# Score and mask matmuls of a recurrence over 128 rows instead of 64 and 40

## The chip, the core and the metric

The kernel runs on one core of a Trainium2 chip. The metric is the device time of one execution in microseconds (us). TensorE (PE in the profile) does the matmuls, VectorE (DVE), ScalarE (ACT) and GpSimd (POOL) the rest; SyncE (SP) issues most DMAs. A matmul has a stationary operand, which a weight load (PEld) puts into the array, and a moving one, whose columns stream past it; it contracts over the rows (partitions) that both operands occupy, 128 at most.

## The reference, cut to what matters

Two transformer blocks follow each other (512 tokens, width 1024, float32). The change lies in the first mixer of the first block, a gated recurrence (mLSTM) with 8 heads, query and key width 64, value width 128:

```python
def mlstm_chunkwise(q, k, v, i_pre, f_pre):
    logf = jax.nn.log_sigmoid(gate(f_pre))
    ig = gate(i_pre)
    b = jnp.cumsum(logf, axis=-1)
    ...
    D = jnp.where(causal, b[..., :, None] - b[..., None, :] + ig[..., None, :], -jnp.inf)
    m_t = jnp.maximum(b_inter, jnp.max(D, axis=-1))
    P = jnp.exp(D - m_t[..., None]) * jnp.einsum('bhctk,bhcsk->bhcts', q, k)
    ...
    h = num / jnp.maximum(jnp.abs(den), jnp.exp(-m_t))[..., None]
```

Queries and keys are projections of the input that go through a causal convolution of four taps and a SiLU. A second mixer (stick-breaking attention), the output projection and an MLP end the first block; a sparse attention is the second.

## The kernel before, in words

The kernel treats the recurrence as one masked attention over all 512 tokens, without chunks. A head's scores, transposed (key s in the rows, query t in the columns), come in four key blocks `sb` of 128 rows and 512, 384, 256 and 128 columns. Float32 accuracy is had by splitting an operand into a rounded part and a rest. `qs` holds in 64 of its rows the head's rounded queries and in the other 64 the rests (L513, L514); `kh` holds the rounded keys twice (L515, L516); `kl` the rests of the keys, in 64 rows only (L517). A score block is two matmuls into one bank of PSUM: `kh` with `qs` over 128 rows (L529), then `kl` with the rounded queries over 64 rows (L530). The mask factor `E` is an exponential (L524) of a running maximum that is first spread over all partitions: a matmul over 40 rows (L519) of `mst`, whose rows 0 to 7 and 32 to 39 hold the maximum of the eight heads, rounded and rest, with a column of the selector `s8` repeated 128 times.

DVE multiplies scores and mask (L531, recorded at its helper's line L298); then follow 10 matmuls with the values per head (L544), DVE's copy of their sum (L546, in the trace "spare"), the norm (squares on ACT L549, a power on POOL and a product on DVE, both recorded at L301 as "mnr", a scaling on ACT L560) and a transposition (L484).

The loop runs over four pairs `j` of heads, `e` = 0 and 1 in each. A pair's projections (L341 to L343, 24 matmuls each for q and for k) stand on PE among the previous pair's scores, and during the last pairs those of the next mixer (L374 to L376). Each engine has its own queue and works it in order; Tile's scheduler set those orders when the kernel was built. Three steps bind them: the score blocks alternate between two banks (`sc2`), so a pair's third block waits for DVE's product on the first; a value sum takes the one bank `av`, so the next waits for the copy L546; the scores of a pair wait for ACT's copies of the keys (L515, L516), which stand behind convolution and SiLU. Weights come by DMA on SP's queue three tiles ahead.

`qs`, `kh`, `kl` of e = 0 are three tiles of the pool `pm`; those of e = 1 are slices of a tile `AT`, taken anew in each pair. The stores of the bias tables (L735, L736), of which the change's name speaks, stand on GpSimd's queue in this kernel already.

Of the kernel before, what the change touches and what calls it, by code (L numbers as in the profile page):

```python
# [8 lines left out]
F32 = mybir.dt.float32  # L9
F32R = mybir.dt.float32r  # L10
AF = mybir.ActivationFunctionType
OP = mybir.AluOpType
# [3 lines left out]
T = 512  # L16
# [237 lines left out]
def tile_blocks(ctx, tc, x, xt, wts, prm, cst, table, post_g, w2k, w2v, out):  # L254
    nc = tc.nc
    v, s, g, pe, sy = nc.vector, nc.scalar, nc.gpsimd, nc.tensor, nc.sync
# [17 lines left out]
    ident = glob.tile([128, 128], F32, name="ident")  # L274
# [10 lines left out]
    def col(base, k, rows=128):  # L285
        return pr[0:rows, base + k:base + k + 1]
# [10 lines left out]
    def stt(out_, a, sc, b, op0, op1):  # L297
        v.scalar_tensor_tensor(out_, a, sc, b, op0, op1)  # L298

    def tt(out_, a, b, op=OP.mult, eng=None):  # L300
        (eng or v).tensor_tensor(out_, a, b, op)  # L301
# [26 lines left out]
    def act_tiles(kt):  # L328
        h = glob.tile([128, T], F32R, name=f"ah{kt}", tag="ah", bufs=8)
        l = glob.tile([128, T], F32R, name=f"al{kt}", tag="al", bufs=8)  # L330
        return h, l
# [65 lines left out]
    def first_mixer():  # L397
        with tc.tile_pool(name="pa", bufs=1) as pa:
            pj, sc, mx, tp, av = ring(0, 1, 2, 3), ring(4), ring(5), ring(6), ring(7)
            acts = []  # L400
            for kt in range(KT):
                xk = pa.tile([128, T], F32, name="xk", tag="w2", bufs=2)
                sy.dma_start(xk, xt[128 * kt:128 * kt + 128, :])
                h, l = act_tiles(kt)
# [14 lines left out]
            with tc.tile_pool(name="pm", bufs=1) as pm:  # L419
# [6 lines left out]
                def values(h0, n, w):  # L426
                    def evac(tb, ps):
                        s.activation(VA[:, tb, h0:h0 + n, 0:128],
                                     ps[:, 0:128 * n].rearrange("p (a b) -> p a b", a=n), AF.Identity,
                                     scale=rs[:, tb:tb + 1])  # L430
                        if w > 128 * n:
                            s.activation(gt[:, tb, :].rearrange("p (a b) -> p a b", b=8)[:, 0:5:4, :],
                                         ps[:, 128 * n:128 * n + 16].rearrange("p (a b) -> p a b", a=2),
                                         AF.Identity, scale=rs[:, tb:tb + 1])
                    emit(gen_n(pj, acts, evac, w=w))
# [20 lines left out]
                um = pa.tile([40, T], F32, name="um", tag="ke", bufs=2)  # L456
# [2 lines left out]
                M = pa.tile([8, T], F32, name="M", tag="w2b", bufs=2)  # L459
                v.tensor_tensor_scan(M, um[0:8, :], um[0:8, :], 0.0, OP.max, OP.bypass)  # L460
                stt(um[32:40, :], F, -1.0, M, OP.mult, OP.subtract)
                mst = pa.tile([40, T], F32R, name="mst", tag="be", bufs=2)
                v.tensor_copy(mst, um)
                v.tensor_copy(mst[0:8, :], M)
                tt(mst[32:40, :], M, mst[0:8, :].bitcast(F32), OP.subtract)
                s8 = pa.tile([40, 8], F32R, name="s8")
                tt(s8, ident[0:40, 0:8], ident[0:40, 32:40], OP.add)
                values(6, 2, 256)
                pst = sc()
                for tb in range(4):  # L470
# [10 lines left out]
                def flip_head(h, num):  # L481
                    pst = tp()
                    for tb in range(4):
                        pe.transpose(pst[:, 128 * tb:128 * tb + 128], num[:, tb, 0:128], ident)  # L484
                    s.activation(ha[:, h, :], pst, AF.Identity, scale=col(P_GML, h))

                for j in range(4):
                    qk = []
                    for i in range(2):
                        ps = proj_t(pj3, acts)  # L490
                        xp = pm.tile([128, T + 4], F32, name="xp", tag="xp", bufs=2)
                        v.memset(xp[:, 0:3], 0.0)
                        tt(xp[:, 3:T + 3], ps, R)
                        y = pm.tile([128, T], F32, name="y", tag="cv", bufs=2)
                        cb = P_CONV + 4 * (4 * i + j)
                        s.activation(y, xp[:, 0:T], AF.Identity, scale=pr[:, cb:cb + 1])
                        for t in range(1, 4):
                            stt(y, xp[:, t:t + T], pr[:, cb + t:cb + t + 1], y, OP.mult, OP.add)
                        th = xp[:, 0:T]
                        s.activation(th, y, AF.Tanh, scale=0.5)  # L500
                        stt(y, th, 1.0, y, OP.add, OP.mult)
                        qk.append(y)
                    q_, k_ = qk
                    for e in range(2):
                        h = 2 * j + e
                        rows = slice(64 * e, 64 * e + 64)
                        other = slice(64 - 64 * e, 128 - 64 * e)
                        if e == 0:
                            qs, kh, kl = (pm.tile([128, T], F32R, name="st", tag=f"st{i}", bufs=1) for i in range(3))
                        else:  # L510
                            st = pa.tile([128, 4, T], F32R, name="AT", tag="AT", bufs=1)
                            qs, kh, kl = (st[:, i, :] for i in range(3))
                        s.copy(qs[rows, :], q_[rows, :])  # L513
                        tt(qs[other, :], q_[rows, :], qs[rows, :].bitcast(F32), OP.subtract)  # L514
                        s.copy(kh[rows, :], k_[rows, :])  # L515
                        s.copy(kh[other, :], k_[rows, :])  # L516
                        tt(kl[rows, :], k_[rows, :], kh[rows, :].bitcast(F32), OP.subtract)  # L517
                        mb = mx()
                        pe.matmul(mb, s8[:, h:h + 1].to_broadcast([40, 128]), mst, start=True, stop=True)  # L519
                        PT = []  # L520
                        for sb in range(4):
                            n = T - 128 * sb
                            E = pm.tile([128, n], F32, name="E", tag=f"E{sb}", bufs=2)
                            s.activation(E, mb[:, 128 * sb:T], AF.Exp, scale=-1.0, bias=un[:, sb, h:h + 1])  # L524
                            g.affine_select(E[:, 0:128], E[:, 0:128], pattern=[[1, 128]], compare_op=OP.is_ge,
                                            fill=0.0, base=0, channel_multiplier=-1)
                            S = sc2()
                            ks = slice(128 * sb, 128 * sb + 128)
                            pe.matmul(S[:, 0:n], kh[:, ks], qs[:, 128 * sb:T], start=True, stop=False)  # L529
                            last = pe.matmul(S[:, 0:n], kl[rows, ks], qs[rows, 128 * sb:T], start=False, stop=True)  # L530
                            stt(E, S[:, 0:n], 0.125 / 4, E, OP.mult, OP.mult)  # L531
                            PT.append(E)
                        if len(late) > LATE:
                            with tc.issue_after(last.ins):
                                flip_head(*late.pop(0))
                        num = spare[:, 516 * (h % NUMS):516 * (h % NUMS) + 516].rearrange("p (a b) -> p a b", a=4)
                        sq = small([128, 4], "sq")
                        for half in range(2):
                            o = av()
                            o2 = o[:, 0:258].rearrange("p (a b) -> p a b", a=2)  # L540
                            for i in range(2):
                                tb = 2 * half + i
                                for sb in range(tb + 1):
                                    pe.matmul(o2[:, i, :], PT[sb][:, 128 * (tb - sb):128 * (tb - sb) + 128],  # L544
                                              VA[:, sb, h, 0:129], start=(sb == 0), stop=(sb == tb))
                            v.tensor_copy(num[:, 2 * half:2 * half + 2, :], o2)  # L546
                        jk = glob.tile([128, 128], F32, name="jk", tag="dg", bufs=2)
                        for tb in range(4):
                            s.activation(jk, num[:, tb, 0:128], AF.Square, accum_out=sq[:, tb:tb + 1])  # L549
                        den = small([128, 4], "den")  # L550
                        stt(den, num[:, :, 128], -1.0, num[:, :, 128], OP.mult, OP.max)
                        tt(den, den, enm[:, :, h], OP.max)
                        v.reciprocal(den, den)
                        r2 = small([128, 4], "r2")
                        tt(r2, den, den)
                        tt(r2, r2, sq)
                        f = rsqrt_mean(r2, 128, "mn", 4)
                        tt(f, f, den)
                        for tb in range(4):
                            s.activation(num[:, tb, 0:128], num[:, tb, 0:128], AF.Identity, scale=f[:, tb:tb + 1])  # L560
                        late.append((h, num))
# [843 lines left out]
```

## Time and profile before

| what | value |
|---|---|
| time, median of 3 runs | 1387.51 us (1386.82 to 1389.72) |
| profiled execution, its own time | 1387.11 us |
| its span | 1385.2 us (mean granted clock 0.994) |
| PE busy | 1331.9 us, 96% |
| DVE busy | 809.2 us, 58% |
| ACT busy | 650.8 us, 47% |
| stretch of the recurrence's heads | 66.91 to 158 us |

The profile is of one execution; times in it are microseconds from the span's start. A matmul's end is modelled, and successive matmuls overlap in the records, so that pace is read from the differences of their starts.

### The profile page before, as it was taken

The numbers are of one execution on the slowest core, as the hardware profiler recorded it, in microseconds if no ns is written. First come the engines' busy times: TensorE is split into PE (matmuls) and PEld (weight loads), VectorE is DVE, ScalarE is ACT, GpSimd is POOL, SyncE is SP. The second block draws the span as 40 slices with busy tenths as digits, with TensorE's granted clock in tenths as the row PEclk, the third lists the DMA queues.
The fourth block names the chain that finished last, engine by engine and source line by source line (L and its number), as shares of the span: only waits on it lengthen the run. The fifth ranks groups of instructions, "written<-read, shape, count | busy, mean of one in ns | idle before, by whom it ended". The sixth has DMA issues, their size and how long they took to land.

```text
span 1385.2 us, 17815 instructions
## 1 busy us (share of the span) xinstructions
PE 1331.9 (96%) x6622; PEld 1087.3 (78%) x6622; DVE 809.2 (58%) x1596; ACT 650.8 (47%) x1273; POOL 264.5 (19%) x235
## 2 busy tenths in 40 slices
PE   9999999999999999999999999899788999999898
PEld 7977787868686888888888888788677878777776
DVE  4678535556667535342233323545988998988823
ACT  6577634443434326351135512344546656665522
POOL 0022101010101000000000000144536342323352
PEclk9999999999999999999999999999999999999999
DMA  7411221213121424762332234323223122121132
GB/s 236 135 43 49 61 92 61 91 47 97 56 91 48 149 78 132 117 187 91 97 100 92 96 100 124 111 61 121 84 63 111 50 61 68 48 70 47 52 122 76
DMA packets 40695, 125.31 MB, mean 90 GB/s; under 512 B 4528, under 2 KB 9184, under 8 KB 40352
## 3 DMA queue, kind: packets, MB, share of 16 engines
q1 hardware_dynamic: 39696, 119.98, 27.3%
q0 software_dynamic: 912, 4.19, 2.3%
q8 instruction: 52, 0.85, 0.3%
q14 instruction: 35, 0.29, 0.1%
HBM read 115.77 MB, written 8.39 MB: 90 GB/s over the span
## 4 chain that ended last, share of the span: by engine, by line
PE 60%; issue 15%; DVE 15%; ACT 5%; POOL 3%; DMA 1%; SPq 0%; POOLq 0%; DVEq 0%; ACTq 0%
PE b L375 9%; PE b L374 9%; PE b L376 9%; PE b L341 8%; PE b L342 8%; PE b L343 8%; DVE P L295 3%; DVE b L1173 2%; DVE ptall L301 2%; ACT wh L172 1%; PE b L824 1%; ACT P L1177 1%; PE b L1208 1%; PE b L544 1%; PE b L1192 1%
## 5 line engine op out<-in xcount | busy, mean ns | idle before, releaser
L172 ACT CAST wh<-wr 128x1024 fp32r<-128x1024 f32 (+3 forms) x204 | 207.9, 1020 | 399.0 <-PE b L376 223.4
L174 DVE TENSOR_TENSOR wl<-wr,wh 128x1024 fp32r<-128x1024 f32 (+2 forms) x142 | 169.5, 1195 | 296.8 <-ACT wh L172 296.4
L341 PE MATMUL b<-ah,wh 128*128 128x512 f32 x808 | 329.4, 408 | 0.4 <-DVE q L298 0.3
L343 PE MATMUL b<-ah,wl 128*128 128x512 f32 x808 | 317.5, 393 | 0.0
L342 PE MATMUL b<-al,wh 128*128 128x512 f32 x808 | 317.2, 393 | 0.0
L343 PEld LDWEIGHTS b<-ah,wl 128*128 128x128 f32 x808 | 152.2, 188 | 33.5 <-issue 0.8
L341 PEld LDWEIGHTS b<-ah,wh 128*128 128x128 f32 x808 | 152.5, 189 | 27.8 <-issue 1.0
L174 POOL TENSOR_TENSOR wl<-wr,wh 128x1024 fp32r<-128x1024 f32 (+1 forms) x62 | 143.6, 2320 | 157.7 <-ACT wh L172 148.0
L342 PEld LDWEIGHTS b<-al,wh 128*128 128x128 f32 x808 | 152.8, 189 | 24.1 <-issue 0.5
L374 PE MATMUL b<-wh,ah 128*128 128x512 f32 (+3 forms) x352 | 125.8, 359 | 1.4 <-ACT ah L308 0.9
L376 PE MATMUL b<-wh,al 128*128 128x512 f32 (+3 forms) x352 | 125.5, 357 | 0.1
L375 PE MATMUL b<-wl,ah 128*128 128x512 f32 (+3 forms) x352 | 125.3, 356 | 0.1
L1177 ACT ACTIVATE P<-b,nm 128x128 f32<-128x128 f32 (+3 forms) x128 | 67.5, 528 | 105.2 <-DVE nm L1173 102.8
L375 PE MATMUL b<-wl,hh 128*128 128x512 f32 x256 | 102.1, 399 | 0.0
L374 PE MATMUL b<-wh,hh 128*128 128x512 f32 x256 | 100.9, 394 | 0.0
L376 PE MATMUL b<-wh,hl 128*128 128x512 f32 x256 | 100.4, 392 | 0.0
L295 DVE TENSOR_SCALAR P<-P,rd,gn 128x128 f32<-128x128 f32 (+3 forms) x128 | 93.7, 732 | 2.4
L374 PEld LDWEIGHTS b<-wh,ah 128*128 128x128 f32 x352 | 66.2, 188 | 9.9 <-ACT ah L308 1.3
L376 PEld LDWEIGHTS b<-wh,al 128*128 128x128 f32 x352 | 66.4, 189 | 8.8 <-DVE al L298 0.5
L375 PEld LDWEIGHTS b<-wl,ah 128*128 128x128 f32 x352 | 66.4, 189 | 8.4 <-DVE wl L174 0.5
L1192 PE MATMUL b<-ident,P 128*128 128x128 f32 x320 | 56.7, 275 | 12.7 <-DVE ptall L301 10.4
L301 POOL TENSOR_TENSOR rsr<-rsm,mhalf 128x2 f32<-128x2 f32 (+1 forms) x3 | 2.4, 806 | 334.6 <-DVE rsm L295 334.6
(288 smaller groups left out, 2214.1 us busy)
## 6 DMA issues: line engine op xcount, KB each, us to landing
wr<-in_wts_dram SPq DMA_DIRECT2D x188, 512.0 KB, 3.6
bt_d<-tr POOLq DMA_DIRECT2D x4, 768.0 KB, 21.9
wr<-in_wts_dram SPq DMA_DIRECT2D x8, 280.0 KB, 2.6
xk<-in_xt_dram SPq DMA_DIRECT2D x8, 256.0 KB, 4.1
xn<-in_x_dram SPq DMA_DIRECT2D x4, 512.0 KB, 5.6
xbig<-in_x_dram SPq DMA_DIRECT2D x1, 2048.0 KB, 9.6
x_d<-xbig SPq DMA_DIRECT2D x8, 256.0 KB, 3.0
bt<-bt_d SPq DMA_DIRECT2D x8, 256.0 KB, 2.8
```

Source lines behind the costliest of these rows:

```text
L172: nc.scalar.copy(hi, raw)
L174: eng.tensor_tensor(lo, raw, hi.bitcast(F32), OP.subtract)
L295: (eng or v).tensor_scalar(out_, in_, s1, s2, op0, op1)
L301: (eng or v).tensor_tensor(out_, a, b, op)
L341: pe.matmul(o, a, ah, start=(kt == 0), stop=False)
L342: pe.matmul(o, a, al, start=False, stop=False)
L343: pe.matmul(o, b, ah, start=False, stop=(kt == KT - 1))
L374: pe.matmul(o, ah[:, tsl], a, start=(kk == 0 and k == 0), stop=False)
L375: pe.matmul(o, ah[:, tsl], b, start=False, stop=False)
L376: W.last = pe.matmul(o, al[:, tsl], a, start=False, stop=end)
L1177: latest[0] = s.activation(P[:, 0:n], S[:, 0:n], AF.Exp, bias=nm, scale=-1.0, accum_out=rd)
L1192: pe.transpose(pst[:, 128 * sb:128 * sb + 128], P[:, 128 * sb:128 * sb + 128], ident)
```

## The change

`mst` and `s8` become tiles of 128 rows; `mst` is set to zero once, rows 0 to 39 are then written as before, and the mask matmul contracts over all 128. `kl` becomes for each `e` one tile that lives through the whole loop: its 64 unused rows are set to zero once ahead of the loop, and the second score matmul takes all 128 rows of `kl` and `qs`. The tile `AT` is therefore taken once, ahead of the loop. Bias stores are where they were.

```diff
-                mst = pa.tile([40, T], F32R, name="mst", tag="be", bufs=2)
-                v.tensor_copy(mst, um)
+                mst = pa.tile([128, T], F32R, name="mst", tag="be", bufs=2)
+                v.memset(mst.bitcast(F32), 0.0)
+                v.tensor_copy(mst[0:40, :], um)
...
-                s8 = pa.tile([40, 8], F32R, name="s8")
-                tt(s8, ident[0:40, 0:8], ident[0:40, 32:40], OP.add)
+                s8 = pa.tile([128, 8], F32R, name="s8")
+                tt(s8, ident[:, 0:8], ident[:, 32:40], OP.add)
...
+                st = pa.tile([128, 4, T], F32R, name="AT", tag="AT", bufs=1)
+                kz = [pm.tile([128, T], F32R, name="kz"), st[:, 2, :]]
+                for e in range(2):
+                    v.memset(kz[e][64 - 64 * e:128 - 64 * e, :].bitcast(F32), 0.0)
...
-                            qs, kh, kl = (pm.tile([128, T], F32R, name="st", tag=f"st{i}", bufs=1) for i in range(3))
+                            qs, kh = (pm.tile([128, T], F32R, name="st", tag=f"st{i}", bufs=1) for i in range(2))
...
-                            st = pa.tile([128, 4, T], F32R, name="AT", tag="AT", bufs=1)
-                            qs, kh, kl = (st[:, i, :] for i in range(3))
+                            qs, kh = (st[:, i, :] for i in range(2))
+                        kl = kz[e]
...
-                        pe.matmul(mb, s8[:, h:h + 1].to_broadcast([40, 128]), mst, start=True, stop=True)
+                        pe.matmul(mb, s8[:, h:h + 1].to_broadcast([128, 128]), mst, start=True, stop=True)
...
-                            last = pe.matmul(S[:, 0:n], kl[rows, ks], qs[rows, 128 * sb:T], start=False, stop=True)
+                            last = pe.matmul(S[:, 0:n], kl[:, ks], qs[:, 128 * sb:T], start=False, stop=True)
```

PE's order of before, in the scores of head 0 (b_730 and b_737 are the score banks, b_896 the bank of a projection):

```order
389 L529 MATMUL b_730<-st 128x256
390 L530 MATMUL b_730<-st 128x256
391 L544 MATMUL b_742<-VA,E 128x129 x2
392 L529 MATMUL b_737<-st 128x128
393 L530 MATMUL b_737<-st 128x128
```

And the same place after the change, where a line's number is higher by six:

```order
389 L535 MATMUL b_734<-st 128x256
390 L536 MATMUL b_734<-st,kz 128x256
391 L550 MATMUL b_746<-VA,E 128x129 x2
392 L535 MATMUL b_741<-st 128x128
393 L536 MATMUL b_741<-st,kz 128x128
```

Nothing moves there: apart from the numbers of buffers and lines, PE's queue is the same from end to end, and so are those of ACT, POOL and SP. Only DVE's queue has new rows, at its start (al_94 is the rest of the first input tile):

```order
5 L457 MEMSET um 40x512
6 L463 MEMSET mst 128x512
7 L491 MEMSET kz 64x512
8 L491 MEMSET AT 64x512
9 L498 MEMSET xp 128x3 x2
10 L293 TENSOR_SCALAR gqs<-pr 128x1
11 L635 MEMSET inc 128x1 x2
12 L298 SCALAR_TENSOR_TENSOR al_94<-xk,pr,ah_93 128x512
```

Three memsets stand ahead of the first work on the input, and a small product (gqs) passes another two.

## Rows read from the trace of the kernel before

**Rows 1.** The page's first part: busy us, share of the span, instructions.

```profile
PE 1331.9 (96%) x6622; PEld 1087.3 (78%) x6622; DVE 809.2 (58%) x1596; ACT 650.8 (47%) x1273; POOL 264.5 (19%) x235
```

**Rows 2.** Windows: length, busy us per engine, granted clock, DMA share, GB/s.

```profile
66.91:158.00 91.09, 88.88 (x437) 66.15 (x436) 70.01 (x162) 66.67 (x171) 22.26 (x39) 1.00 0.13 41
```

**Rows 3.** PE's waits, 66.91 to 158: total us, times, longest.

```profile
PE b L529 <- ACT st L516: 2.1, 3, 0.8
```

**Rows 4.** Timeline of PE around the first mask matmul: start, duration (us).

```profile
66.91 0.39 PE L343 MATMUL b<-ah,wl 128*128 128x512 f32 x1
67.23 0.50 PE L519 MATMUL b<-mst,s 40*128 40x512 f32 x1
67.66 0.50 PE L341 MATMUL b<-ah,wh 128*128 128x512 f32 x1
68.00 0.40 PE L342 MATMUL b<-al,wh 128*128 128x512 f32 x1
68.24 0.40 PE L343 MATMUL b<-ah,wl 128*128 128x512 f32 x1
```

**Rows 5.** Timeline of PE in the first three score blocks of head 0.

```profile
76.46 0.39 PE L343 MATMUL b<-ah,wl 128*128 128x512 f32 x1
76.68 0.40 PE L529 MATMUL b<-st 128*128 128x512 f32 x1
77.01 0.50 PE L530 MATMUL b<-st 64*128 64x512 f32 x1
77.44 0.44 PE L529 MATMUL b<-st 128*128 128x384 f32 x1
77.81 0.44 PE L530 MATMUL b<-st 64*128 64x384 f32 x1
78.18 0.50 PE L341 MATMUL b<-ah,wh 128*128 128x512 f32 x1
78.52 0.39 PE L342 MATMUL b<-al,wh 128*128 128x512 f32 x1
...
79.21 0.28 PE L529 MATMUL b<-st 128*128 128x256 f32 x1
79.42 0.38 PE L530 MATMUL b<-st 64*128 64x256 f32 x1
79.73 0.71 PE L544 MATMUL b<-VA,E 128*128 128x129 f32 x4
```

**Rows 6.** Timeline of PE in an undisturbed run of 256 columns.

```profile
54.80 0.28 PE L376 MATMUL b<-wh,al 128*128 128x256 f32 x1
54.92 0.28 PE L374 MATMUL b<-wh,ah 128*128 128x256 f32 x1
```

**Rows 7.** DVE's waits, 76.46 to 143.85: total us, times, longest.

```profile
DVE mnr L301 <- POOL mnr L301: 4.5, 5, 1.3
DVE E L298 <- PE b L530: 4.2, 11, 1.0
DVE spare L546 <- PE b L544: 1.2, 3, 0.5
```

**Rows 8.** The chain of waits ahead of the second pair's scores: start, us, what.

```profile
94.88 1.51 POOL mnr L301
...
100.59 0.62 ACT st L516
```

**Rows 9.** Timeline of DVE in the last pair.

```profile
145.36 0.16 DVE L301 TENSOR_TENSOR mnr<-mnr,den 128x4 f32<-128x4 f32 x1 [1.12 <-POOL mnr L301]
```

**Rows 10.** Timeline of DVE at the start of the span.

```profile
1.38 0.48 DVE L457 MEMSET um<- 40x512 f32 x1
...
4.89 0.75 DVE L298 SCALAR_TENSOR_TENSOR al<-xk,pr,ah 128x512 fp32r<-128x512 f32 x1 [2.03 <-ACT ah L308]
```

**Rows 11.** PE's waits, 860 to 905, when the second block begins.

```profile
PE b L824 <- DVE al L298: 3.1, 1, 3.1
```

**Rows 12.** The window behind that wait, columns as in rows 2.

```profile
890.00:895.00 5.00, 5.00 (x32) 5.00 (x32) 2.00 (x5) 1.39 (x4) 0.00 (x0) 0.67 0.61 180
```

## The prediction

> **What bounds the kernel now.** I read the page's busy times first, then the windows of the stretch that the change touches, then PE's waits there, then PE's timeline start by start, and last what DVE waits for. PE is busy 96% of the span [rows 1] and 88.9 of the 91.1 us of the recurrence's heads [rows 2]; its own waits for data in that stretch are three, 2.1 us together [rows 3]. So PE sets the pace, but not alone: DVE is busy 70.0 and ACT 66.7 of the same 91.1 us [rows 2]. "Busy" says little here, because a matmul's recorded end is modelled. The starts say more. In a run of full matmuls with 512 columns they stand 0.22 to 0.24 us apart (68.00 to 68.24, 76.46 to 76.68) [rows 4, 5]; I use 0.23. Around a matmul with 40 or 64 rows they do not.
>
> **What the change removes: the price of a matmul on fewer rows.** Around the first mask matmul the starts go 66.91, 67.23, 67.66, 68.00 [rows 4]: 0.32, 0.43 and 0.34, together 1.09 where three full ones take 0.69. That is 0.40 for one L519; there are 8 (one per head), so 3.2 us. In the first two score blocks of head 0 [rows 5] the starts from 76.46 to 78.52 span 2.06 for six matmuls: four with 512 columns and two with 384. At full pace these would take 4 x 0.23 + 2 x 0.17 (0.23 scaled by 384/512, an estimate) = 1.26, so two L530 cost 0.80. In the third block 79.21, 79.42, 79.73 give 0.52 for two matmuls of 256 columns; undisturbed ones stand 0.12 apart [rows 6], so the price is 0.28. The fourth (128 columns) I take at the same 0.28. A head's four L530 cost 1.36, eight heads 10.9. With the mask matmuls, **14.1 us** of PE's time is spent on 40 switches between row counts.
>
> That a full-row matmul of equal columns has no such price is read from rows of the same kind: the first L529 of rows 5, with the same type, the same banks and 128 rows, comes 0.22 after its neighbour. PE's order is unchanged, so after the change every one of the 40 stands between full-row matmuls (only the four transpositions of the gates, L471, keep 40 rows, ahead of this stretch). A first long matmul behind short ones may still lose some 0.1 (68.00 comes 0.34 after 67.66 without a switch of its own); over the eight heads I leave 1 us for that. The price of the zeros themselves on PE is nothing, since a matmul's pace goes by columns and these are the same.
>
> **What comes through to the end.** PE arrives earlier; do its inputs? The three waits of rows 3 are the test. Each is the first score matmul of a pair that waits for ACT's second key copy. Followed back, that copy at 100.59 stands behind a power on POOL, a scaling on ACT and the convolution on DVE [rows 8], a chain of some 10 us that no matmul shortens. So what PE saves between a pair's last value sums and the next pair's first scores is lost at the wait, and what it saves among a pair's scores counts only as far as DVE moves up with it. DVE moves up by the time that it now idles for PE: between 76.46 and 143.85, 4.2 us for L530 (11 times) and 1.2 for the value sums [rows 7], **5.4 us** for three pairs. The rest of DVE's idle time, 4.5 us for POOL's powers [rows 7], stays. PE saves more than that in three pairs (6 heads x 1.36 = 8.2), so DVE is the shorter of the two and I take 5.4.
>
> The last pair has no next pair behind it; the work that follows on PE (projections of the next mixer) needs nothing of the chain. There PE's own price counts: 2 heads x 1.36 = 2.7. Of it, the two first L530 (0.80) are lost: the third score block needs the bank that DVE's first product frees, and DVE reaches that only behind its product at 145.36, for which it has waited 1.12 us for POOL [rows 9]. That leaves **1.9**. Ahead of the first pair, L519 at 67.23 lets ACT start its exponentials 0.1 earlier, and the chain with it; the rest of the two early L519 runs into the first scores' wait for the key copies: **0.1**.
>
> **What the change adds.** Three memsets ahead of DVE's first work. A memset of 512 columns took 0.48 [rows 10]; the three, at that, 1.4, and they end before 1.9 + 1.4 = 3.3, gqs and two tiny ones behind them. DVE's first real work starts at 4.89 and DVE idled 2.03 before it [rows 10], so the cost is nothing; without that cover it would be 1.4. From the other side: at 0.75 each, DVE's pass over 512 columns with arithmetic in it (the second of rows 10), they take 2.25 and delay the first tile by 0.2. They cannot gain. The selector s8 is wider in rows only, and DVE's time for it goes by its 8 columns: nothing. `AT` taken once instead of four times removes no wait: the rows that are rewritten are still those that the last scores have read. The zero rows are written once, and no DMA, ACT, POOL or SP instruction moves; the bias stores in the change's name do not move either.
>
> **Sum.** 5.4 + 1.9 + 0.1 = 7.4 us less than the profiled execution's 1387.1 us (span 1385.2 and 1.9 around it), so 1379.7. The median of the runs is 0.4 above the profiled execution; I predict **1380 us**. Behind 158 us everything moves up together: PE goes on with full-row matmuls, and the DMAs of weights are set off by the work that consumes them, with a DMA share of 0.13 here [rows 2].
>
> **Rivals.**
>
> *PE takes nearly all of it.* If DVE and ACT have more slack than their waits show (the order of their queues lets a convolution step slip into the time that an idle PE wait took), all 14.1 less the 1 us behind short matmuls comes back: 1374. For it: PE is the busiest engine and waited only 2.1 us. Against it: DVE at 70 of 91.1 us would have to do the same work in 78. Chance 0.15, with what lies between.
>
> *The wait takes the gain.* The three first-score waits grow by what PE saves, because the chain through POOL's power and ACT's scaling has a fixed length and DVE's idle time turns from waits for PE into waits for POOL, which are 4.5 us already [rows 7]. Then only the last pair's 1.9 and the 0.1 count: 1385.5, within the bound. Chance 0.11.
>
> *Slower by the clock.* Early in the second block PE waited 3.1 us for DVE [rows 11], and the granted clock of the window from 890 to 895 was then 0.67 [rows 12]: of its 5 us, 3.3 at half speed, the 1.2 GHz level, a loss of about 1.7. If the gain turns into waits as in the last rival, each of the three waits grows from some 0.7 to 0.7 + 8.2 / 3 = 3.4, beyond 3.1, and each would cost 1.7: 5.1 lost against 2.0 gained, 1390.6. It decides from waits of about 3 us; the clock was 1.00 throughout the stretch with waits of 0.8 at most [rows 2, 3], and the main forecast leaves the waits near (2.1 + 8.2 - 5.4) / 3 = 1.6 each. Chance 0.02.
>
> *Fewer rows were the cheaper form.* By rows: if the zeros cost as much again as the used rows, that is if a 64-row matmul is worth half a full one, 32 L530 at a mean of 0.16 and 8 L519 at 0.23 would add 0.5 x 5.1 + 0.7 x 1.8 = 3.8 and the time would be 1391.3. The 0.43 behind a 64-row matmul of 512 columns against 0.23 behind a full one [rows 5] speaks against it. Chance 0.01.
> The Trainium skill's page "TensorEngine Tiling (Array Packing)", section "Performance Considerations", is the voice for this rival: it advises row tiling where the contraction is 64 rows or fewer. By its "Theoretical Speedup", up to twice for 64 rows, what the change gives up would be worth the last rival's amount; in this trace no 64-row matmul is faster than a full one, and its section "Key Properties", by which a change of the tiling mode drains the array, is the one that rows 4 and 5 agree with.
>
> That the change does not do what it says I give 0.01: PE's queue shows the second score matmul on `kz` with the same columns.
>
> **How the numbers follow.** The forecast with its own range (5 to 10 us gained, 1377.5 to 1382.5) has 0.70. The range that should hold the time 8 times in 10 reaches 1375.5 to 1384: below it lies the larger half of the first rival, above it the second and the slower ones. What can be told from no change is 0.2%, 2.8 us: faster is below 1384.7. That takes the forecast and the first rival and a little of the second, 0.87; within it lies most of the second rival and the case without effect, 0.10; slower 0.03.
>
> **What would show it.** Right: starts of the second score matmul and of the mask matmul 0.23 behind and ahead of their neighbours at 512 columns; PE's waits for ACT's key copies grown from 2.1 to some 5 us in all; DVE's waits for the score matmuls and value sums nearly gone between the pairs; the stretch from the first mask matmul to the end of the heads about 7 us shorter, and all later stretches equal. Wrong: gaps of 0.3 to 0.4 that remain around full-row matmuls (then the row count was not the cause); key waits that stay near 2 us with the stretch 11 us or more shorter (first rival); waits above 3 us with a clock below 1.00 (third); a later first matmul (the memsets).

## The result: 10 us faster

| | median us (lowest to highest) | ratio to before, 95% interval |
|---|---|---|
| before, at first | 1387.38 (1386.82 to 1389.72) | |
| after, at first | 1377.25 (1376.83 to 1377.41) | 0.9921 (0.9907 to 0.9936) |
| after, in the runs below | 1377.10 (1375.99 to 1377.89) | 0.9922 (0.9910 to 0.9935) |

The change gives 10.1 us in the first runs and 10.4 in the second, where 7.4 were forecast. The direction is right, and the time lies inside the range that should hold it 8 times in 10 (1375.5 to 1384), but 0.3 us below the forecast's own, narrower range (1377.5 to 1382.5). The page of the changed kernel, which answers to [rows 1]:

```profile
span 1375.5 us, 17818 instructions
PE 1320.0 (96%) x6622; PEld 1085.8 (79%) x6622; DVE 808.2 (59%) x1599; ACT 650.3 (47%) x1273; POOL 265.9 (19%) x235
```

PE has lost 12 us of busy time (1331.9 before) and the span 9.7. PE's timeline around the first mask matmul and in the first score blocks (start, duration; L525 is the mask matmul, L535 and L536 the score matmuls) answers to [rows 4, 5]:

```profile
66.31 0.39 PE L343 MATMUL b<-ah,wl 128*128 128x512 f32 x1
66.54 0.39 PE L525 MATMUL b<-mst,s 128*128 128x512 f32 x1
66.77 0.39 PE L341 MATMUL b<-ah,wh 128*128 128x512 f32 x1
...
75.36 0.50 PE L535 MATMUL b<-st 128*128 128x512 f32 x1
75.70 0.39 PE L536 MATMUL b<-st,kz 128*128 128x512 f32 x1
75.92 0.34 PE L535 MATMUL b<-st 128*128 128x384 f32 x1
76.10 0.34 PE L536 MATMUL b<-st,kz 128*128 128x384 f32 x1
76.28 0.39 PE L341 MATMUL b<-ah,wh 128*128 128x512 f32 x1
```

The gaps are gone: 0.23 on both sides of the mask matmul where 0.32 and 0.43 stood, 0.22 behind the second score matmul with 512 columns (0.43), 0.18 with 384 (0.37). Only the first of the block still takes 0.34, although nothing around it has fewer rows. It comes behind a wait for ACT's second key copy that the list of waits does not count: it starts 0.05 us after that copy has ended, here in the changed kernel:

```profile
74.69 0.62 ACT L522 CAST st<-y 64x512 fp32r<-64x512 f32 x1
```

Where the rest of the price went, the windows and waits of the heads' stretch show. First the windows (length; busy us of PE, PEld, DVE, ACT, POOL; granted clock, DMA share, GB/s): against [rows 2] the whole stretch, then the three pairs from the first scores of the first to those of the last:

```profile
66.54:148.27 81.73, 76.91 (x436) 64.07 (x435) 68.56 (x162) 65.95 (x169) 23.28 (x39) 1.00 0.15 46
75.36:135.85 60.49, 56.60 (x319) 47.12 (x318) 53.08 (x127) 50.03 (x130) 16.21 (x27) 1.00 0.16 50
```

The same three pairs in the kernel before:

```profile
76.68:143.85 67.17, 65.10 (x319) 48.47 (x318) 54.34 (x126) 50.03 (x130) 15.34 (x27) 1.00 0.13 42
```

PE's waits in the stretch after the change, against [rows 3], and then DVE's in the three pairs, against [rows 7]:

```profile
PE b L535 <- ACT st L522: 3.7, 3, 1.5
PE b L535 <- DVE E L298: 0.9, 1, 0.9
```

```profile
DVE mnr L301 <- POOL mnr L301: 4.1, 5, 0.9
...
DVE E L298 <- PE b L536: 0.2, 1, 0.2
DVE spare L552 <- PE b L550: 0.2, 1, 0.2
```

By the list of waits PE now waits 4.6 us instead of 2.1, for the keys' copies and, in the last pair, for DVE's first product. DVE waits 0.4 us for PE instead of 5.4. Behind the stretch everything moves up together: the 251.73 us behind it contain nearly the same busy times in both kernels, first before, then after:

```profile
158.00:409.73 251.73, 246.75 (x1123) 193.75 (x1123) 138.33 (x224) 110.51 (x175) 31.32 (x53) 1.00 0.25 78
```

```profile
148.27:400.00 251.73, 246.75 (x1123) 193.71 (x1123) 138.29 (x224) 110.60 (x176) 31.42 (x53) 1.00 0.26 78
```

### The profile page after: what moved, and what is told of

It is laid out like the page before. It is cut to its first block, busy times and chain, and to the rows that moved or that the text cites. A ratio compares the mean times of both kernels' runs of the same rounds, so it can differ in the third digit from the quotient of the medians.

```text
span 1375.5 us, 17818 instructions
## 1 busy us (share of the span) xinstructions
PE 1320.0 (96%) x6622; PEld 1085.8 (79%) x6622; DVE 808.2 (59%) x1599; ACT 650.3 (47%) x1273; POOL 265.9 (19%) x235
## 4 chain that ended last, share of the span: by engine, by line
PE 60%; DVE 17%; issue 15%; ACT 5%; POOL 2%; DMA 0%; POOLq 0%; SPq 0%; DVEq 0%; ACTq 0%
PE b L375 10%; PE b L376 10%; PE b L374 10%; PE b L341 8%; PE b L342 8%; PE b L343 8%; DVE P L295 4%; DVE b L1179 2%; DVE ptall L301 2%; ACT wh L172 1%; PE b L830 1%; ACT P L1183 1%; PE b L1214 1%; PE b L1198 1%; DVE Pc L301 1%
## 5 line engine op out<-in xcount | busy, mean ns | idle before, releaser
L1198 PE MATMUL b<-ident,P 128*128 128x128 f32 x320 | 56.6, 275 | 12.8 <-DVE ptall L301 10.6
## 6 DMA issues: line engine op xcount, KB each, us to landing
xbig<-in_x_dram SPq DMA_DIRECT2D x1, 2048.0 KB, 10.1
```

What stands on the lines that cost most here:

```text
L1198: pe.transpose(pst[:, 128 * sb:128 * sb + 128], P[:, 128 * sb:128 * sb + 128], ident)
```

## The experiments

The runs of one group share a chip and the runs of the kernel before; the two versions with the short POOL step form a group of their own, in which the kernel before took 1387.18 us, and a ratio compares within its group. In the table the profiles' starts on PE are turned into lengths: from the first mask matmul to the first scores of pair 0, from these to those of the next pairs, and from the last pair's to the last transposition of a head. Two profiles of one kernel agree here within 0.03 us, so that this shows more than the medians do. Before it, by starts, 67.23, 76.68 [rows 4, 5] and

```profile
101.26 0.50 PE L529 MATMUL b<-st 128*128 128x512 f32 x1 [0.81 <-ACT st L516]
126.11 0.49 PE L529 MATMUL b<-st 128*128 128x512 f32 x1 [0.62 <-ACT st L516]
143.85 0.50 PE L529 MATMUL b<-st 128*128 128x512 f32 x1 [0.63 <-ACT st L516]
164.34 0.27 PE L484 MATMUL b<-ident,spare 128*128 128x128 f32 x1
```

and after it

```profile
97.57 0.67 PE L535 MATMUL b<-st 128*128 128x512 f32 x2 [1.06 <-ACT st L522]
120.19 0.51 PE L535 MATMUL b<-st 128*128 128x512 f32 x1 [1.51 <-ACT st L522]
135.85 0.50 PE L535 MATMUL b<-st 128*128 128x512 f32 x1 [1.10 <-ACT st L522]
154.62 0.27 PE L485 MATMUL b<-ident,spare 128*128 128x128 f32 x1
```

| kernel | median us | ratio to before, 95% | to pair 0 | pair 0 | pair 1 | pair 2 | pair 3 | sum |
|---|---|---|---|---|---|---|---|---|
| before | 1387.54 | | 9.45 | 24.58 | 24.85 | 17.74 | 20.49 | 97.11 |
| mask only | 1387.09 | 0.9999 (0.9989 to 1.0010) | 8.83 | 24.45 | 24.45 | 17.74 | 20.50 | 95.97 |
| scores only | 1378.76 | 0.9937 (0.9925 to 0.9949) | 9.45 | 21.92 | 22.92 | 15.66 | 18.75 | 88.70 |
| 72 and 96 rows | 1376.92 | 0.9925 (0.9914 to 0.9937) | 8.84 | 22.19 | 22.60 | 15.66 | 18.75 | 88.04 |
| after, again | 1377.10 | 0.9922 (0.9910 to 0.9935) | 8.83 | 22.19 | 22.62 | 15.66 | 18.76 | 88.06 |
| before, short POOL step | 1384.02 | 0.9977 (0.9968 to 0.9986) | 9.45 | 23.60 | 24.26 | 16.99 | 19.99 | 94.29 |
| after, short POOL step | 1372.83 | 0.9897 (0.9884 to 0.9911) | 8.82 | 21.19 | 21.43 | 14.69 | 17.79 | 83.92 |

The theory: a matmul whose rows fit in half of the array costs PE two switches, and what PE saves counts only as far as DVE moves up and the keys' copies come earlier. Rivals: all of PE's saving counts; any change of the row count costs; the chain to the copies is set by other work than POOL's.

**The two halves of the change.** The mask matmul alone: the edits of `mst`, `s8` and the mask matmul, without those of `kl`. The scores alone: the others.

> Only the mask matmul contracts over 128 rows (8 of the 40 switches between row counts go, 3.2 us of PE's time by the starts); the second score matmul stays at 64 rows. All queues but DVE's memset at the start are as before. Theory (a switch costs PE 0.4 us, but between the first scores of one pair and those of the next a gain counts only as far as DVE moves up): the two early mask matmuls give 0.7, those that stand inside a pair's scores some 0.4 each, those ahead of a pair's first scores nothing: 1.5 to 2 us faster, 1385.4 to 1385.9. Rival (all PE time saved counts): 3.2 us, 1384.2. Rival (the row count is not the cause): 1387.4.

> Only the second score matmul contracts over 128 rows (32 of the 40 switches go, 10.9 us of PE's time); the mask matmul stays at 40 rows. Theory: 10.1 less the 1.5 to 2 of the mask part, so 8 to 8.6 us faster, 1378.8 to 1379.4. Rival (all PE time saved counts, the whole change then being held up elsewhere): its share by PE time, 10.1 x 10.9 / 14.1 = 7.8 us, 1379.6. If the row count is not the cause: 1387.4.

The mask alone cannot be told from no change by its time; its starts show 1.14 us, less than the 1.5 to 2 expected: 0.62 ahead of the first pair, 0.13 and 0.40 in pairs 0 and 1, nothing in pairs 2 and 3, of which the first has one mask matmul and the last none. The rest became waits: PE's waits for the copies grew to 3.3 us in that run. The rival by which all 3.2 us count is out. The scores alone give 8.8 us, just above the theory's 8 to 8.6, and 8.41 by starts. Its interval, 7.1 to 10.4 us, holds the rival's 7.8 too, so this run's time does not decide between the two.

**Which row counts cost.**

```diff
-pe.matmul(mb, s8[:, h:h + 1].to_broadcast([128, 128]), mst, start=True, stop=True)
+pe.matmul(mb, s8[0:72, h:h + 1].to_broadcast([72, 128]), mst[0:72, :], start=True, stop=True)
...
-last = pe.matmul(S[:, 0:n], kl[:, ks], qs[:, 128 * sb:T], start=False, stop=True)
+last = pe.matmul(S[:, 0:n], kl[0:128 - 32 * (1 - e), ks], qs[0:128 - 32 * (1 - e), 128 * sb:T], ...)
```

> The changed kernel, but the mask matmul contracts over 72 rows and the second score matmul of the even heads over 96 (zeros in the unused ones as before); odd heads stay at 128. All queues are those of the changed kernel. Theory A (the price comes with a matmul whose rows fit in half of the array, 64 or fewer): no price at 72 and 96 rows, starts 0.23 us apart, time of the changed kernel, 1377.3. Rival B (any change of the row count costs): 24 of 40 switches are back, some 6 us, 1383.

> The changed kernel again, beside the others on the same chip. 1377.3 by its earlier runs. What it tells: whether PE's wait of 0.9 us at 25 us, which the profile of before has and that of after has not, belongs to the change (then it is missing here too, and present in the mask-only and key-only kernels only if their memsets matter) or comes and goes by the run.

Theory A holds: the times are equal, and PE's timeline of this run has full pace around 72 and 96 rows:

```profile
66.36 0.39 PE L343 MATMUL b<-ah,wl 128*128 128x512 f32 x1
66.58 0.40 PE L525 MATMUL b<-mst,s 72*128 72x512 f32 x1
66.82 0.40 PE L341 MATMUL b<-ah,wh 128*128 128x512 f32 x1
...
75.75 0.40 PE L536 MATMUL b<-st,kz 96*128 96x512 f32 x1
75.99 0.34 PE L535 MATMUL b<-st 128*128 128x384 f32 x1
```

It is not the change of the row count that costs, but going to 64 rows or fewer (40 and 64 do, 72 and 96 do not; what lies between 64 and 72 was not tried) and back. That it is the going and not the small matmul itself, one place of the kernel before shows, where two of them stand side by side (the second has 384 columns):

```profile
102.00 0.39 PE L342 MATMUL b<-al,wh 128*128 128x512 f32 x1
102.31 0.67 PE L530 MATMUL b<-st 64*128 64x512 f32 x2
102.91 0.50 PE L343 MATMUL b<-ah,wl 128*128 128x512 f32 x1
103.25 0.40 PE L341 MATMUL b<-ah,wh 128*128 128x512 f32 x1
```

From 102.00 to 103.25 are 1.25 us where four full matmuls of these columns would take 3 x 0.23 + 0.17 = 0.86: 0.39 for both together, as much as for one alone.

The weight loads (PEld) show where the time goes. Among full matmuls of 512 columns a load starts some 0.22 us ahead of its own matmul, while the one before it still runs. The load of the mask matmul did not, nor did that of the full matmul behind it, in the kernel before (in brackets the idle time of the engine; "issue" is time in which it waited for nothing that the profile shows):

```profile
67.23 0.18 PEld L519 LDWEIGHTS b<-mst,s 40*128 40x128 f32 x1 [0.35 <-issue]
67.65 0.19 PEld L341 LDWEIGHTS b<-ah,wh 128*128 128x128 f32 x1 [0.25 <-issue]
67.76 0.19 PEld L342 LDWEIGHTS b<-al,wh 128*128 128x128 f32 x1
```

Both start with their matmuls, at 67.23 and 67.66; the next one is again 0.24 ahead of its matmul at 68.00. The mask matmul's load after the change, and then over 72 rows, each 0.22 ahead:

```profile
66.31 0.19 PEld L525 LDWEIGHTS b<-mst,s 128*128 128x128 f32 x1
```

```profile
66.36 0.19 PEld L525 LDWEIGHTS b<-mst,s 72*128 72x128 f32 x1
```

And the loads of the second of the two small matmuls side by side, 0.23 ahead of its matmul at 102.65, and of the full one behind it, which starts with its own:

```profile
102.42 0.19 PEld L530 LDWEIGHTS b<-st 64*128 64x128 f32 x1
102.91 0.19 PEld L343 LDWEIGHTS b<-ah,wl 128*128 128x128 f32 x1 [0.31 <-issue]
```

So it is in all 39 places of the kernel before where PE goes from full to small, and in all 39 where it goes back: no load starts more than 0.01 us ahead of its matmul. At 512 columns two lost leads of 0.22 come to about the price of 0.40. How the rest of a price comes about with fewer columns, and what holds a load back, no run shows.

The wait at 25 us was meant to tell something of the memsets, and does not: PE's two waits for the first tiles come to 0.4 us in this run, 1.2 in the first profile of the changed kernel and 1.3 in the scores-only one. Two profiles of the same kernel thus differ by 0.8 us there; that the landing of the first DMAs sets it is likely, but not shown. By that, 0.6 of the 9.7 us between the two first profiles lie ahead of the mask matmul (67.23 against 66.54, of which 0.09 is the change) and belong to no step of it.

**What holds the rest.** In the changed kernel and in the kernel before, the power in the heads' norm on POOL becomes a multiplication of the same shape. It leaves out the inverse square root of the norm; the queues keep their order.

```diff
-        tt(r, m, mhalf[:, 0:cols], OP.pow, eng=g)
+        tt(r, m, mhalf[:, 0:cols], OP.mult if name == "mn" else OP.pow, eng=g)
```

> The changed kernel with the power of the heads' norm on POOL replaced by a multiplication of the same shape (leaves out the inverse square root of the norm; every queue's order as in the changed kernel). DVE waits 4.1 us for these powers in three pairs, and the keys' copies stand behind them. Theory (what PE saves beyond DVE's pace is lost in the waits for the keys' copies, whose chain runs through POOL's power): PE's waits for them and for DVE's product, 4.6 us together, shrink by half or more; 2 to 4 us faster than the changed kernel, 1373 to 1375. Rival (the chain is set by ACT's and DVE's own work, POOL's part is hidden): within 0.5 us of 1377.1.

> The same replacement in the kernel before (leaves out the inverse square root of the norm; every queue's order as before). Theory: there PE waits only 2.1 us for keys, so at most these come back: 1385.5 to 1386.7, and the change is worth more with the shorter chain than without, 11 to 13 us between this run and the one beside it instead of 10. Rival: within 0.5 us of the kernel before, and the difference stays 10.

POOL's instructions on that tile in the changed kernel (ns, least, median, most), and in the run with the multiplication:

```profile
L301 POOL TENSOR_TENSOR mnr<-mnm,mhalf x8: 1007/1016/1505, 85.8 to 151.9; 128x4 f32<-128x4 f32 x8
```

```profile
L301 POOL TENSOR_TENSOR mnr<-mnm,mhalf x8: 198/202/697, 84.8 to 146.9; 128x4 f32<-128x4 f32 x8
```

PE's waits in the heads' stretch of that run:

```profile
PE b L535 <- ACT st L522: 0.9, 3, 0.4
```

0.8 us less in each of 8 powers takes PE's waits from 4.6 to 0.9 us, and the median lies 14.4 us below the kernel before of its group where the changed kernel's lies 10.4 below: some 4 us, 4.1 by the starts. POOL's power is in the chain that holds the keys back, as the theory says. In the kernel before the same edit gives 3.2 us (2.8 by the starts), more than the 2.1 that the list gives as PE's waits there and than I expected; the list then has no wait of PE in the stretch. So with the chain short the change is worth 11.2 us by the medians, at the low edge of the 11 to 13 forecast, and 10.4 by the starts, below it.

What the 40 switches cost PE can be read interval by interval, since PE's order is the same in both kernels. From the first mask matmul to the last transposition of a head 94 intervals between starts are shorter after the change by over 0.04 us, by 12.5 us together; 14 are longer, by 3.6 (the growth of the recorded waits is 2.5 of that), and the whole falls by 9.0. With the short POOL step the same count gives 12.4 us shorter and 2.2 longer.

**Three versions that did not win.** The second key copy on POOL, `g.tensor_copy(kh[other, :], k_[rows, :])` instead of ACT's:

> A version: the changed kernel with the second copy of the rounded keys, on which each pair's first scores wait, on POOL instead of ACT (the scheduler orders PE's, DVE's and ACT's queues anew). Theory: the copy runs beside ACT's first one instead of behind it (0.6 us each), ACT loses 8 x 0.6 us of work, so the waits for keys shorten by up to 0.5 each: 1375 to 1376.5. Rival (POOL is slower at it, and a queue's new order costs as much): 1377 to 1380.

The small product behind the power on POOL, `tt(f, f, den, eng=g)`, in the changed kernel and in the one before:

> A version: the changed kernel with the small product behind POOL's power (mnr) on POOL too, so that DVE's queue no longer holds an instruction that waits about 1 us for POOL in each of 8 heads (5.9 us of DVE's time in this stretch). The scheduler orders the queues anew. Theory (DVE's waits for POOL are what delays convolution and keys): PE's waits for the keys' copies shrink, 1373.5 to 1375.5, at best the 1372.8 of the run with a short POOL instruction. Rival (the chain from value sums to keys is the power itself, not DVE's blocked queue): 1376.5 to 1378.

> The same move of the small product to POOL in the kernel before (PE's, ACT's and POOL's queues are those of the version beside it). Theory: PE waits little there, so it gains less than the version does, 1385 to 1387, and the full-row matmuls are worth 10.5 to 12 us between these two. Rival: the difference stays 10 or falls below.

The norm with fewer steps:

```diff
-                            s.activation(jk, num[:, tb, 0:128], AF.Square, accum_out=sq[:, tb:tb + 1])
+                            s.activation(jk, num[:, tb, 0:128], AF.Square, scale=128.0 ** -0.5,
+                                         accum_out=sq[:, tb:tb + 1])
...
-                        v.reciprocal(den, den)
-                        tt(r2, den, den)
-                        tt(r2, r2, sq)
-                        f = rsqrt_mean(r2, 128, "mn", 4)
-                        tt(f, f, den)
+                        stt(r2, den, EPS, den, OP.mult, OP.mult)
+                        tt(r2, r2, sq, OP.add)
+                        f = small([128, 4], "mnr")
+                        tt(f, r2, mhalf[:, 0:4], OP.pow, eng=g)
```

> A version: the changed kernel with the norm of the heads written as (sq/128 + eps*d*d)^-0.5, d the denominator, which is the same value with 4 small DVE instructions per head instead of 7 and no product on DVE behind POOL's power. The scheduler orders the queues anew, much as in the run with the product on POOL (1383.9). Theory A (that run was slow because its chain got longer: power and product one behind the other on POOL, 11 us of ACT's waits for them): the chain is now shorter than in the changed kernel, PE's waits shrink, 1374 to 1376.5. Theory B (it was slow because of the new order of the queues, whatever the chain): 1381 to 1384 again.

The copy on POOL took 1378.47 us, in its rival's range; the product on POOL 1383.89, in the kernel before 1398.07 (0.9969 and 1.0076 of before, intervals 0.9957 to 0.9981 and 1.0063 to 1.0089); the short norm 1380.12. In all of them the scheduler gave PE another order, so that none is a clean test of its step. For the product both expectations fell. DVE no longer waits for POOL, but ACT does, and PE with it. ACT's largest wait in the changed kernel with the product on POOL, and PE's two largest:

```profile
ACT spare L566 <- POOL mnr L301: 11.0, 8, 2.0
```

```profile
PE b L525 <- ACT E L530: 4.6, 3, 1.9
PE b L535 <- ACT st L522: 4.5, 3, 2.2
```

Between these two kernels the change is worth 14.2 us, above the 10.5 to 12 of the expectation. The granted clock has a part in that: by the windows it was at half, the 1.2 GHz level, for 10.2 us of the stretch in the kernel before with this product and for 3.4 in the changed one. If half of those times is lost, an estimate, that is 5.1 against 1.7 us, and without it the difference would be 10.8.

The short norm lies between its two theories; chain and order may both have a part, and no run separates them. Of the versions that leave nothing out the changed kernel is the fastest.

## Why the prediction was right, and where its sizes were off

**The price of a switch: right in kind, 14.1 us was 1.6 too much.** The starts stand where they were forecast, 0.22 to 0.23 apart. Interval by interval the 40 switches cost PE 12.5 us, where the forecast had 14.1 less the 1 that I left for the first long matmul behind short ones. By the same count the scores-only run gives 10.6 (10.9 forecast) and the mask-only run 2.6 (3.2). A price taken from one place was multiplied, although the next interval at some of the others is long anyhow: behind a wait (0.34 at 75.36 above) or behind short matmuls. In the other direction, the 0.28 for 256 columns left out the interval behind the next matmul, which is shorter by 0.10 after the change.

**What lies between the scores and the next pair: right.** PE's waits for the copies grew, from 2.1 to 3.7 where some 4.9 were forecast; PE's saving behind a pair's last value sums went into them, which the mask-only run shows by itself. The first rival, by which nearly all of PE's saving counts, is out: by the starts, 9.0 of the 12.5 us came through. The second, by which the waits take it all, is out too.

**Three pairs: 5.4 forecast, 6.7 measured** (67.17 to 60.49). DVE's idle time for PE went as forecast, 5.4 to 0.4: 5.0. The term left out the rest: DVE's waits for POOL fell by 0.4 (4.5 to 4.1), and its busy time by 1.26 (54.34 to 53.08) with the same work: the instructions' durations in the two windows sum to 60.4 and 60.3 us, but 7.2 us of them overlap after the change and 6.1 before. The timeline shows how: an instruction that waits for nothing starts before the one ahead of it has ended by its record, as the second does here in the kernel before:

```profile
79.91 0.43 DVE L298 SCALAR_TENSOR_TENSOR E<-b,E 128x256 f32<-128x256 f32 x1 [0.99 <-PE b L530]
80.25 0.74 DVE L298 SCALAR_TENSOR_TENSOR y<-xp,pr,y 128x512 f32<-128x512 f32 x1
```

80.25 is 0.09 before 79.91 + 0.43. Of the 14 waits for PE that the prediction counted 12 are gone; 12 x 0.09 is 1.1. So a wait that goes gave back its idle time and some 0.09 more. That is read from the rows and was not tested by a run of its own.

**The last pair: 1.9 forecast, 1.72 measured** (20.49 to 18.77), by the step as told: the 0.9 that PE now waits for DVE's first product is the 0.80 that the forecast wrote off there.

**Ahead of the first pair: 0.1 forecast, 0.62 measured.** I let the two early mask matmuls' saving run into the wait for the keys' copies. In the kernel before, the first scores stand at 76.68, and the profile has no wait there; the second copy had ended at 76.11:

```profile
75.49 0.62 ACT L516 CAST st<-y 64x512 fp32r<-64x512 f32 x1
```

I took the half microsecond between them for the delay of the signal. The second and later pairs start 0.05 behind their copies, so it was slack; after the change the first pair starts 0.05 behind its copy too.

**The memsets: nothing**, as forecast. They took 0.48 us each, and DVE still idled 1.32 us (2.03 before) ahead of its first work on the input, which starts at 5.09 instead of 4.89 us.

These terms with their measured sizes are 0.09 + 0.62 + 6.68 + 1.72 = 9.1 us. The medians give 10.1 to 10.4, with an interval of 9.0 to 12.5 us for the second measurement; what the last microsecond is, if anything, stays open. The forecast was 7.4, so its terms were too small by 1.7 us, of which the three pairs are 1.3 and the stretch ahead of them 0.5.

**The slower rivals.** No recorded wait of the changed kernel's heads exceeds 1.5 us and its clock stays at 1.00 in the stretch, so the clock took nothing. But the length of one wait, about 3 us in the forecast, is not what decides. With the product on POOL, PE waited 2.2 us for the copies from 120 to 122, and the clock of the next window was below full, 1.2 GHz for a part of it:

```profile
125.00:130.00 5.00, 5.00 (x35) 4.78 (x34) 4.04 (x9) 1.95 (x6) 0.00 (x0) 0.82 0.00 0
```

In the kernel before with this product the clock fell behind a wait of 1.23 us and stayed full behind one of 2.02:

```profile
100.81 0.49 PE L529 MATMUL b<-st 128*128 128x512 f32 x1 [1.23 <-ACT st L516]
129.77 0.50 PE L529 MATMUL b<-st 128*128 128x512 f32 x1 [2.02 <-ACT st L516]
```

```profile
105.00:110.00 5.00, 5.00 (x16) 3.58 (x15) 1.80 (x4) 0.81 (x4) 0.00 (x0) 0.58 0.32 105
130.00:135.00 5.00, 5.00 (x24) 3.40 (x23) 3.87 (x7) 3.32 (x6) 0.29 (x1) 1.00 0.00 0
```

That fewer rows are the cheaper form is refuted by the starts: a lone 64-row matmul cost more than a full one at every width. The Trainium skill's page "TensorEngine Tiling (Array Packing)" has both voices: its advice of row tiling at 64 rows or fewer ("Performance Considerations") speaks for the short contractions of the kernel before, its sentence that a change of the tiling mode drains the engine ("Key Properties") gives a reason for their price. The 0.4 us for a lone small matmul among full ones, and the loads that start late on both sides of it, agree with the second; that a matmul over 64 rows or fewer runs in another mode, no run shows.

## What to carry to other kernels

Look at the starts of matmuls, not at their busy time: a lone matmul over 64 rows or fewer among full ones cost 0.28 to 0.40 us here, and zeros in the unused rows, written once, made it free; 72 rows did as well as 128. Then ask how far the engine that works next can move up: a saving on PE counted about as far as DVE had been idle for PE, and the rest became waits. And where a scheduler sets the order, a small edit elsewhere (a product on another engine) also changes that order and can cost more than it saves, here some 6.5 us.

## What the runs showed that I had not expected

- A power on GpSimd over 128 x 4 numbers takes 1.0 us, a multiplication of the same shape 0.2; eight of them, off the busiest engine, were worth some 4 us of the whole.
- The price of small row counts ends between 64 and 72 rows, and it goes with weight loads that start with their matmul instead of 0.22 us ahead of it.
- DVE gives back more than its idle time when a wait goes, some 0.09 us each by the rows.
- The granted clock fell behind a wait of 1.23 us and stayed full behind one of 2.02.
